# One layer of a hybrid decoder: norm chains and transformed operands issued in small steps between products, gate and up results moved to VectorE, weight sums to GpSimd

## The chip, the cores and the metric

One core of a Trainium2 chip runs the whole program. The metric is device microseconds of that core for one execution, the median of three runs. TensorE (PE) does the matrix products, VectorE (DVE), ScalarE (ACT) and GpSimd (POOL) the elementwise work, and SyncE's queue (SP) issues every DMA.

## The reference

One decoder layer on 1088 tokens (a prompt of 1024 and 8 sequences of 8 new tokens), model width 1024, in float32. Cut to what matters here:

```python
mix = concat([o_att, o_ssm]) @ w_out          # 2048 -> 1024
x = x + rmsnorm(mix, g_post_mix)
f = rmsnorm(x, g_pre_ffn)
f = (silu(f @ w_gate) * (f @ w_up)) @ w_down  # 1024 -> 2816 -> 1024
x = x + rmsnorm(f, g_post_ffn)
```

Ahead of it stand one combined input projection, sliding-window attention with sinks and a Mamba-2 scan with a gated group norm. The change touches none of those but the group norm of the last tokens.

## The kernel before, in words

Activations lie transposed, features on partitions and tokens along the free axis, in three chunks of 384, 384 and 320 tokens (CH). Each float32 operand is split into a high part (an ACT copy that rounds) and a low part (a subtraction on POOL or DVE), and each product is three matmuls (high by high, high by low, low by high).

PE's order is the order in which the program is written out: generators yield the PE time that they want to see pass, in microseconds of matmul columns, and `weave` hands out that much of a filler (the big products) before it goes on with the mixer. The other engines' queues and SP's are ordered by a planner from the same program: an operation goes out when it can, by priority of its place in the program, and `high_priority` moves it ahead. Each queue then runs strictly in its order.

The stages that matter here, in order:

- **Attention, out-projection op(0), op(1), op(2)** (L1000): one product per chunk and 128 features, 61 us for a chunk of 384 columns at the pace that the generators count.
- **gate(2)** (L953): the gated group norm of chunk 2. After a gap of 18 us, `rms` sums squares with matmuls by a column of ones (`g2st`), takes the power on POOL, builds a diagonal on DVE (`g2d`), and after a gap of 5.0 broadcasts it with matmuls (`g2R`).
- **chain(c)** (L1029) for each chunk: `rms` over the mixer's result (`pm`), eight k-steps on 128 features (scale L1039, add of x L1040, store to DRAM, square and sum), a gap of 21.76, a second `rms` (`pf`). Chunks 0 and 1 meet in chain(1): the gate and up products of the two are computed by Strassen-Winograd, seven half-size products in place of eight. Its operands B11, B21, B22 and T1 to T4 are built and split there (L1063 to L1083). Chunk 2 is multiplied plainly: chain(2) splits its operand f2.
- **first_up** (L1314), the filler while chain(1) and chain(2) run: `gu_early` gives the B11 and B21 products of the column pairs 0 to 2 (names eg.., eu..), then whole column pairs without their chunk-2 part until chain(2) is done. `part` counts those.
- **gu_unit** (L1140): one block of gate or up weights. It loads four quarter blocks (r11, r21, r22, r12; four raw slots in all), forms the sums S1 to S4 of them (`ssum`; S3 and S4 stand behind the T1 product), splits each (`lot`), and accumulates the products in the banks pa, pb, pc (Winograd) and qa, qb (plain). The bank pb takes T2, T3 and T4 in turn: before each of the last two, DVE must have added the bank into u2 or u3 (L1206, L1227). Results 1 and 2 are added and multiplied by POOL for the larger part (L1228, L1231).
- Then the pairs without chunk-2 part get it (`wino=False`), with h loaded back for **down** (L1345), and **fin(c)** (L1359) norms, adds x and stores.

Of the kernel before, what the change touches and what calls it, by code (L numbers as in the profile page):

```python
# [16 lines left out]
P = 128  # L17
# [18 lines left out]
def hybrid_layer(ctx, tc, A):  # L36
# [145 lines left out]

    def rms(groups, n, inv, name, gap, keep=None):

# [17 lines left out]
        for q in range(len(groups)):  # L202
            Rp = ps("o", name + "R")
            for b, off in enumerate(bl):
                t.matmul(Rp[:, off:off + P], lhsT=ones, rhs=dgs[q][:, b, :], start=True, stop=True)
            with tc.high_priority():
                if keep is None:
                    R = sp.tile([P, n], F32, tag="rs_R", bufs=2, name=name + "R")
                else:
                    R = sp.tile([P, n], F32, name=name + "Rk")  # L210
                    keep.append(R)
                s.copy(R, Rp[:, :n])
                Rs.append(R)
            if q + 1 < len(groups):
                yield 0.51
# [736 lines left out]

    def gate(c, gap=6.0):  # L953

# [15 lines left out]
        yield gap  # L970
        Rs = yield from rms([[Z.t[:, 0, :]] for Y, Z in yz], n, 1.0 / 512, "g%d" % c, 5.0)
        S = Split.__new__(Split)
# [56 lines left out]
    def chain(c, mt, acc, kp):  # L1029
        c0, n = CH[c]  # L1030
        yield 6.8
        R, = yield from rms([[acc]], n, 1.0 / DM, "pm%d" % c, 4.0)
        acc = kp.tile([P, n], F32, tag="acc1", bufs=1, name="acc1")
        acc2 = kp.tile([P, n], F32, tag="acc2", bufs=1, name="acc2")
        for k in range(8):
            xr = kp.tile([P, n], F32, tag="xr", bufs=2, name="xr")
            dma(xr, A["xT"][:, k, c0:c0 + n])
            e, a = (g, acc2) if k % 2 else (v, acc)
            v.scalar_tensor_tensor(mt[:, k, :], mt[:, k, :], vec[:, V_GPM + k:V_GPM + k + 1], R, ALU.mult, ALU.mult)  # L1039
            e.tensor_add(mt[:, k, :], mt[:, k, :], xr)  # L1040
            dma(x2_scr[:, k, c0:c0 + n], mt[:, k, :])
            sumsq(a, mt[:, k, :], k // 2, n, e)
        if c == 1:
            for q, name in enumerate(("B11", "B21")):
                h, l = Half(0, name + "h"), Half(0, name + "l")
                slots[name] = (h, l)
                hilo(name, h.t, l.t)
                for k in range(4):
                    split(h.t, l.t, k, mix[0][:, 4 * q + k, :], g)
            done.add("B1")  # L1050
        yield 21.76
        R, = yield from rms([[acc, acc2]], n, 1.0 / DM, "pf%d" % c, 6.8)

# [7 lines left out]
        elif c == 1:  # L1061
# [6 lines left out]
            for k in range(4):  # L1068
                v.tensor_sub(t1[:, k, :], scaled(k), m0[:, k, :])
            for k in range(4):  # L1070
                split(h.t, l.t, k, scaled(4 + k), g)
                v.tensor_sub(t3[:, k, :], mt[:, 4 + k, :], mt[:, k, :])
                v.tensor_sub(t2[:, k, :], mt[:, 4 + k, :], t1[:, k, :])
                g.tensor_sub(t4[:, k, :], m0[:, 4 + k, :], t2[:, k, :])
            while "op2" not in done:
                yield 1.0
            for name, x, e in (("T2", t2, v), ("T1", t1, v), ("T3", t3, g), ("T4", t4, v)):
                h, l = Half(c, name + "h"), Half(c, name + "l")
                slots[name] = (h, l)
                hilo(name, h.t, l.t)  # L1080
                for k in range(0, 4, 2):
                    s.copy(h.t[:, k:k + 2, :], x[:, k:k + 2, :])
                    e.tensor_sub(l.t[:, k:k + 2, :], x[:, k:k + 2, :], fr(h.t[:, k:k + 2, :]))  # L1083
        else:
            h, l = [fpool.tile([P, 8, n], F32R, tag="F", bufs=3, name="f2" + j) for j in "hl"]
            for k in range(8):
                split(h, l, k, scaled(k), g if k % 2 else v)
            for q in range(2):
                hilo("F%d" % q, h[:, 4 * q:4 * q + 4], l[:, 4 * q:4 * q + 4])
# [50 lines left out]
    def gu_unit(gp, src, j, up, sgs, wino, plain):  # L1140
# [4 lines left out]
        with tc.high_priority(offset=500):  # L1145
            for q, i in ((11, 0), (21, 0), (22, 1), (12, 1)) if wino else ((11, 0), (12, 1), (22, 1), (21, 0)):
                r[q] = wp.tile([P, 4, P], F32, tag="raw", bufs=4, name="%sr%d" % (nm, q))
                wdma[0] = dma(r[q], src[2 * j + q // 20][:, 4 * i:4 * i + 4, :]).ins

        def ssum(i, x, y, sub):  # L1150
            with tc.high_priority(offset=500):
                S[i] = gp.tile([P, 4, P], F32, tag="sraw", bufs=4, name="%sS%d" % (nm, i))
                (v.tensor_sub if sub else v.tensor_add)(S[i], x, y)

# [7 lines left out]
        def out(i, m, c, e, put):  # L1162

            c0, nc_ = CH[c]
            with tc.high_priority():
                if not up:
                    sg = gp.tile([P, nc_], F32, tag="sg2" if c == 2 else "sg", bufs=2 if c == 2 else 4, name=nm + "sg")
                    x = put(sg)
# [16 lines left out]
        if wino:  # L1185
            pa, pb, pc = ps("mm", nm + "pa") if j not in early else None, ps("s", nm + "pb"), ps("t", nm + "pc")
            ssum(1, r[21], r[22], False)
            ssum(2, S[1], r[11], True)
        pre = j in early
        if plain or not pre:  # L1190
# [10 lines left out]
        if wino:  # L1201
# [8 lines left out]
            with tc.high_priority():  # L1210
                s.copy(p5, pc[:, :n])
            ssum(3, r[11], r[21], True)
            ssum(4, r[12], S[2], True)
        if plain or not pre:
# [7 lines left out]
        if wino:  # L1222
# [3 lines left out]
            with tc.high_priority():  # L1226
                v.tensor_add(u3, p1, pb[:, :n])  # L1227
            out(1, 1, 1, g, add(g, u3, p5, u3))  # L1228
            w = lot(S[4], "s4", v)
            yield from prod(pc, n, w, "B22")  # L1230
            out(2, 0, 1, g, add(v, u2, pc[:, :n], u2))  # L1231
        w = lot(r[22], 22)
# [68 lines left out]
    def gate2():  # L1301
        while "op0" not in done:
            yield 1.0
        yield from gate(2, 18.0)

    with pool("chain") as kp:
# [3 lines left out]
        with pool("xl") as xl, pool("gu") as gp:  # L1310
# [27 lines left out]
            for j in range(part[0] + 1):  # L1338
                run(gu_pair(gp, j, wino=False))
                next(hl)  # L1340
                next(hl, None)
            run(hl)

    with pool("down") as dp:
# [14 lines left out]
        def fin(c, Y, accs):  # L1359
            c0, n = CH[c]  # L1360

            def x2_load(m):
                x2 = dp.tile([P, n], F32, tag="x2", bufs=4, name="x2_%d" % m)
                dma(x2, x2_scr[:, m, c0:c0 + n])
                return x2
            x2 = [x2_load(m) for m in range(4)]
            R, = yield from rms([accs], n, 1.0 / DM, "fin%d" % c, 0.0)
            for m in range(8):
# [3 lines left out]
                dma(A["o_y"][:, m, c0:c0 + n], xv)  # L1372
                if m < 4:
                    x2.append(x2_load(m + 4))

        fi = None
        for c, (c0, n) in enumerate(CH):
            Y = dp.tile([P, 8, n], F32, tag="Y", bufs=2, name="Y%d" % c)
            accs = [sp.tile([P, n], F32, tag="acc", bufs=2, name="acc")]
            for m in range(8):  # L1380
# [5 lines left out]
                if m == 2 and c < 2:  # L1386
                    run(h_load(dp, c + 1, range(3), c == 0))
                with tc.high_priority():
                    s.copy(Y[:, m, :], o[:, :n])
                    if c == 2 and m > 5:  # L1390
                        accs.append(stage(n, "sq"))
                        s.activation(accs[-1], Y[:, m, :], AF.Square)
                    else:
                        sumsq(accs[0], Y[:, m, :], m, n, v if c == 2 else g)
            for h in held[c]:
                h.free()
            if c < 2:
                run(h_load(dp, c + 1, range(3, 6), c == 1))
            fi = fin(c, Y, accs)
        finish(fi)  # L1400
# [115 lines left out]
```

## Time and profile before

| | |
|---|---|
| median of three runs | 1731.97 us (1728.89 to 1734.25) |
| the profiled execution's own time | 1738.02 us |
| its span, first to last instruction | 1736.1 us |
| busy in the span: PE, POOL, DVE, ACT | 1615.1, 864.4, 964.6, 754.3 us |
| mean granted clock of PE | 0.967 of full speed |

Rows of the profile are of that one execution. A wait is named by the engine that ended it. The granted clock has two levels, 1.2 and 2.4 GHz, shown as 0.5 and 1.0 of full speed; a mean between them is a mixture in time.

### The profile page before, as it was taken

The numbers are of one execution on the slowest core, as the hardware profiler recorded it, in microseconds if no ns is written. First come the engines' busy times: TensorE is split into PE (matmuls) and PEld (weight loads), VectorE is DVE, ScalarE is ACT, GpSimd is POOL, SyncE is SP. The second block draws the span as 40 slices with busy tenths as digits, with TensorE's granted clock in tenths as the row PEclk, the third lists the DMA queues.
The fourth block names the chain that finished last, engine by engine and source line by source line (L and its number), as shares of the span: only waits on it lengthen the run. The fifth ranks groups of instructions, "written<-read, shape, count | busy, mean of one in ns | idle before, by whom it ended". The sixth has DMA issues, their size and how long they took to land.

```text
span 1736.1 us, 27321 instructions
## 1 busy us (share of the span) xinstructions
PE 1615.1 (93%) x9695; PEld 1516.1 (87%) x9695; DVE 964.6 (56%) x1807; ACT 754.3 (43%) x1602; POOL 864.4 (50%) x682
## 2 busy tenths in 40 slices
PE   9999999999789989898996879999999999999996
PEld 6889988878677867898996769999999999999996
DVE  6796768663588878355568743333333342144242
ACT  5242344431576676454544323333333344453442
POOL 5462366665553343234558545444444455556563
PEclk9999999999999999988998989999999999999998
DMA  5122565565552341543463432222222257566463
GB/s 186 32 85 101 152 171 154 151 189 189 147 156 81 93 144 57 167 149 118 130 196 95 134 123 85 75 75 75 73 77 75 75 160 223 157 207 203 143 200 103
DMA packets 180832, 226.10 MB, mean 130 GB/s; under 512 B 21784, under 2 KB 122136, under 8 KB 180664
## 3 DMA queue, kind: packets, MB, share of 16 engines
q1 hardware_dynamic: 180696, 224.37, 41.8%
q8 instruction: 76, 1.25, 0.3%
q14 instruction: 60, 0.49, 0.1%
HBM read 177.99 MB, written 48.54 MB: 130 GB/s over the span
## 4 chain that ended last, share of the span: by engine, by line
PE 58%; DVE 9%; POOL 5%; issue 4%; DMA 4%; ACT 3%; SPq 1%; POOLq 0%; DVEq 0%; ACTq 0%
PE od L1356 5%; PE od L1354 5%; PE od L1355 5%; PE ip L131 2%; PE op L131 2%; PE ip L132 2%; PE ip L133 2%; PE op L133 2%; PE op L132 2%; DMA xr<-in_xT 1%; DVE a_0S L742 1%; DVE gy L982 1%; PE a_0o L820 1%; DMA hs<-h_scr 1%; DVE a_1S L794 1%
## 5 line engine op out<-in xcount | busy, mean ns | idle before, releaser
L115 POOL TENSOR_TENSOR wi_1l<-wi_1r,wi_1h 128x512 fp32r<-128x512 f32 x40 | 56.1, 1405 | 72.5 <-ACT wi_1h L114 67.2
L115 POOL TENSOR_TENSOR wi_0l<-wi_0r,wi_0h 128x512 fp32r<-128x512 f32 x40 | 58.3, 1460 | 31.0 <-ACT wi_0h L114 28.4
L115 POOL TENSOR_TENSOR wos_1l<-wos_1r,wos_1h 128x512 fp32r<-128x512 f32 x24 | 33.5, 1397 | 55.9 <-ACT wos_1h L114 46.0
L115 POOL TENSOR_TENSOR woa_1l<-woa_1r,woa_1h 128x512 fp32r<-128x512 f32 x24 | 33.9, 1412 | 52.5 <-ACT woa_1h L114 50.6
L115 DVE TENSOR_TENSOR wd_2l<-wd_2r,wd_2h 128x512 fp32r<-128x512 f32 x24 | 20.0, 832 | 67.3 <-ACT wd_2h L114 63.3
L115 POOL TENSOR_TENSOR wd_3l<-wd_3r,wd_3h 128x512 fp32r<-128x512 f32 x24 | 33.2, 1383 | 46.0 <-ACT wd_3h L114 43.4
L131 PE MATMUL ip<-x1h,wi_0h 128*128 128x384 f32 x128 | 48.0, 375 | 5.1 <-DVE cbuf L362 2.8
L375 DVE SCALAR_TENSOR_TENSOR cacc<-cbuf,vec,cacc 128x1112 f32<-128x1112 f32 x36 | 52.3, 1455 | 0.7
L131 PE MATMUL ip<-x0h,wi_0h 128*128 128x384 f32 x128 | 48.2, 377 | 4.2 <-DVE cbuf L362 3.5
L115 POOL TENSOR_TENSOR wd_0l<-wd_0r,wd_0h 128x512 fp32r<-128x512 f32 x24 | 32.6, 1358 | 32.8 <-ACT wd_0h L114 32.8
L133 PE MATMUL ip<-x0h,wi_0l 128*128 128x384 f32 x128 | 44.3, 346 | 1.5 <-POOL wi_0l L115 1.5
L1017 DVE TENSOR_TENSOR acc<-acc,sq 128x384 f32<-128x384 f32 (+1 forms) x35 | 27.2, 778 | 32.7 <-ACT sq L1016 32.3
L131 PE MATMUL ip<-x0h,wi_1h 128*128 128x384 f32 x128 | 45.3, 354 | 0.0
L131 PE MATMUL ip<-x1h,wi_1h 128*128 128x384 f32 x128 | 44.5, 347 | 0.0
L133 PE MATMUL ip<-x1h,wi_0l 128*128 128x384 f32 x128 | 44.2, 345 | 0.0
L132 PE MATMUL ip<-x0l,wi_0h 128*128 128x384 f32 x128 | 44.1, 344 | 0.0
L132 PE MATMUL ip<-x1l,wi_0h 128*128 128x384 f32 x128 | 44.0, 343 | 0.0
L133 PE MATMUL ip<-x0h,wi_1l 128*128 128x384 f32 x128 | 43.3, 338 | 0.0
L132 PE MATMUL ip<-x0l,wi_1h 128*128 128x384 f32 x128 | 43.3, 338 | 0.0
L133 PE MATMUL ip<-x1h,wi_1l 128*128 128x384 f32 x128 | 43.1, 337 | 0.0
L132 PE MATMUL ip<-x1l,wi_1h 128*128 128x384 f32 x128 | 43.1, 337 | 0.0
L115 DVE TENSOR_TENSOR wd_5l<-wd_5r,wd_5h 128x256 fp32r<-128x256 f32 x24 | 17.3, 721 | 45.1 <-ACT wd_5h L114 45.1
(2821 smaller groups left out, 6511.5 us busy)
## 6 DMA issues: line engine op xcount, KB each, us to landing
wi_0r<-in_w_in SPq DMA_DIRECT2D x40, 256.0 KB
wi_1r<-in_w_in SPq DMA_DIRECT2D x40, 256.0 KB
hs<-h_scr SPq DMA_DIRECT2D x22, 384.0 KB
wos_0r<-in_w_os SPq DMA_DIRECT2D x24, 256.0 KB
wos_1r<-in_w_os SPq DMA_DIRECT2D x24, 256.0 KB
woa_0r<-in_w_oa SPq DMA_DIRECT2D x24, 256.0 KB
woa_1r<-in_w_oa SPq DMA_DIRECT2D x24, 256.0 KB
wd_0r<-in_w_d SPq DMA_DIRECT2D x24, 256.0 KB
```

What stands on the lines that cost most here:

```text
L115: (eng or g).tensor_sub(lo, raw, fr(hi))
L131: t.matmul(out, lhsT=wh, rhs=xh, start=k == 0, stop=False)
L132: t.matmul(out, lhsT=wh, rhs=xl, start=False, stop=False)
L133: t.matmul(out, lhsT=wl, rhs=xh, start=False, stop=k == n - 1)
L375: v.scalar_tensor_tensor(acc[:, :L], buf[:, k:k + L], vec[:, cw + k:cw + k + 1], acc[:, :L], ALU.mult, ALU.add)
L742: v.tensor_scalar_mul(w, w, den[:, h:h + 1])
L794: v.tensor_tensor_reduce(Sms[e][:, gi, :W], sq_[:, a, :W], cst[:, mcol:mcol + W], 1.0, -3.0e38, ALU.add, ALU.max, mx[:, h:h + 1])
L820: t.matmul(op[HD * e:HD * e + HD, :], lhsT=VT[:, HD * e:HD * e + HD], rhs=PTs[e], start=kt == 0, stop=kt == nk - 1)
L1017: e.tensor_add(acc, acc, sq)
L1354: t.matmul(o[:, :n], lhsT=wh, rhs=xh, start=q + k == 0, stop=False)
L1355: t.matmul(o[:, :n], lhsT=wh, rhs=xl, start=False, stop=False)
L1356: t.matmul(o[:, :n], lhsT=wl, rhs=xh, start=False, stop=q + k == NFF - 1)
```

## The change

The eight k-steps, the building of the T operands and the splits of f2 each get a yield behind them, in place of one gap of 21.76 us; the gaps between the two halves of `rms` are longer for chunk 2. Adds of x for chunks 1 and 2 and the low parts of B22 go from POOL to DVE. In a gate or up unit, results 1 and 2 are added and multiplied on DVE alone, S3 and S4 are formed at the head of the unit on POOL, and r11 and r12 get two slots of their own beside the four. Chunk 2's x is loaded in two pieces during `down`, its last norm factor is read from PSUM, and its last two squares are taken from PSUM.

```diff
-    def rms(groups, n, inv, name, gap, keep=None):
+    def rms(groups, n, inv, name, gap, keep=None, direct=False):
...
                 t.matmul(Rp[:, off:off + P], lhsT=ones, rhs=dgs[q][:, b, :], start=True, stop=True)
+            if direct:
+                Rs.append(Rp[:, :n])
+                continue
             with tc.high_priority():
...
-    def gate(c, gap=6.0):
+    def gate(c, gap=6.0, gap2=5.0):
...
         yield gap
-        Rs = yield from rms([[Z.t[:, 0, :]] for Y, Z in yz], n, 1.0 / 512, "g%d" % c, 5.0)
+        Rs = yield from rms([[Z.t[:, 0, :]] for Y, Z in yz], n, 1.0 / 512, "g%d" % c, gap2)
         S = Split.__new__(Split)
...
         yield 6.8
-        R, = yield from rms([[acc]], n, 1.0 / DM, "pm%d" % c, 4.0)
...
+        R, = yield from rms([[acc]], n, 1.0 / DM, "pm%d" % c, 8.0 if c == 2 else 4.0)
         acc = kp.tile([P, n], F32, tag="acc1", bufs=1, name="acc1")
...
             v.scalar_tensor_tensor(mt[:, k, :], mt[:, k, :], vec[:, V_GPM + k:V_GPM + k + 1], R, ALU.mult, ALU.mult)
-            e.tensor_add(mt[:, k, :], mt[:, k, :], xr)
+            (v if c else e).tensor_add(mt[:, k, :], mt[:, k, :], xr)
             dma(x2_scr[:, k, c0:c0 + n], mt[:, k, :])
             sumsq(a, mt[:, k, :], k // 2, n, e)
+            yield 4.5 if c == 2 else 2.7
         if c == 1:
...
             done.add("B1")
-        yield 21.76
-        R, = yield from rms([[acc, acc2]], n, 1.0 / DM, "pf%d" % c, 6.8)
+        R, = yield from rms([[acc, acc2]], n, 1.0 / DM, "pf%d" % c, 10.0 if c == 2 else 6.8)
...
                 v.tensor_sub(t1[:, k, :], scaled(k), m0[:, k, :])
+                yield 1.2
             for k in range(4):
-                split(h.t, l.t, k, scaled(4 + k), g)
+                split(h.t, l.t, k, scaled(4 + k), v)
                 v.tensor_sub(t3[:, k, :], mt[:, 4 + k, :], mt[:, k, :])
...
                 g.tensor_sub(t4[:, k, :], m0[:, 4 + k, :], t2[:, k, :])
+                yield 2.5
             while "op2" not in done:
...
                     e.tensor_sub(l.t[:, k:k + 2, :], x[:, k:k + 2, :], fr(h.t[:, k:k + 2, :]))
+                    yield 1.2
         else:
...
                 split(h, l, k, scaled(k), g if k % 2 else v)
+                yield 2.0
             for q in range(2):
...
             for q, i in ((11, 0), (21, 0), (22, 1), (12, 1)) if wino else ((11, 0), (12, 1), (22, 1), (21, 0)):
-                r[q] = wp.tile([P, 4, P], F32, tag="raw", bufs=4, name="%sr%d" % (nm, q))
...
+                r[q] = (wp.tile([P, 4, P], F32, tag="raw", bufs=4, name="%sr%d" % (nm, q)) if q > 20 else
+                        gp.tile([P, 4, P], F32, tag="rawx", bufs=2, name="%sr%d" % (nm, q)))
                 wdma[0] = dma(r[q], src[2 * j + q // 20][:, 4 * i:4 * i + 4, :]).ins
...
-        def ssum(i, x, y, sub):
+        def ssum(i, x, y, sub, e=v):
             with tc.high_priority(offset=500):
                 S[i] = gp.tile([P, 4, P], F32, tag="sraw", bufs=4, name="%sS%d" % (nm, i))
-                (v.tensor_sub if sub else v.tensor_add)(S[i], x, y)
+                (e.tensor_sub if sub else e.tensor_add)(S[i], x, y)
...
                 if not up:
-                    sg = gp.tile([P, nc_], F32, tag="sg2" if c == 2 else "sg", bufs=2 if c == 2 else 4, name=nm + "sg")
+                    sg = stage(nc_, nm + "sg") if c == 2 else gp.tile([P, nc_], F32, tag="sg", bufs=4, name=nm + "sg")
                     x = put(sg)
...
             ssum(2, S[1], r[11], True)
+            ssum(4, r[12], S[2], True, g)
+            ssum(3, r[11], r[21], True, g)
         pre = j in early
...
                 s.copy(p5, pc[:, :n])
-            ssum(3, r[11], r[21], True)
-            ssum(4, r[12], S[2], True)
         if plain or not pre:
...
                 v.tensor_add(u3, p1, pb[:, :n])
-            out(1, 1, 1, g, add(g, u3, p5, u3))
+            out(1, 1, 1, v, add(v, u3, p5, u3))
             w = lot(S[4], "s4", v)
             yield from prod(pc, n, w, "B22")
-            out(2, 0, 1, g, add(v, u2, pc[:, :n], u2))
+            out(2, 0, 1, v, add(v, u2, pc[:, :n], u2))
         w = lot(r[22], 22)
...
             yield 1.0
-        yield from gate(2, 18.0)
+        yield from gate(2, 18.0, 9.0)
...
                 run(gu_pair(gp, j, wino=False))
-                next(hl)
+                next(hl, None)
                 next(hl, None)
...
                 return x2
-            x2 = [x2_load(m) for m in range(4)]
-            R, = yield from rms([accs], n, 1.0 / DM, "fin%d" % c, 0.0)
+            if c < 2:
+                x2 = [x2_load(m) for m in range(4)]
+            else:
+                x2 = []
+                for q in range(2):
+                    x_ = Half(c, "x2h%d" % q, F32)
+                    dma(x_.t, x2_scr[:, 4 * q:4 * q + 4, c0:c0 + n])
+                    x2 += [x_.t[:, k, :] for k in range(4)]
+                yield
+            last = c == 2
+            R, = yield from rms([accs], n, 1.0 / DM, "fin%d" % c, 0.0, direct=last)
             for m in range(8):
...
                 dma(A["o_y"][:, m, c0:c0 + n], xv)
-                if m < 4:
+                if m < 4 and c < 2:
                     x2.append(x2_load(m + 4))
...
                     run(h_load(dp, c + 1, range(3), c == 0))
+                if m == 3 and c == 2:
+                    fi = fin(c, Y, accs)
+                    next(fi)
                 with tc.high_priority():
-                    s.copy(Y[:, m, :], o[:, :n])
                     if c == 2 and m > 5:
                         accs.append(stage(n, "sq"))
-                        s.activation(accs[-1], Y[:, m, :], AF.Square)
+                        s.activation(accs[-1], o[:, :n], AF.Square)
+                        v.tensor_copy(Y[:, m, :], o[:, :n])
                     else:
+                        s.copy(Y[:, m, :], o[:, :n])
                         sumsq(accs[0], Y[:, m, :], m, n, v if c == 2 else g)
...
                 run(h_load(dp, c + 1, range(3, 6), c == 1))
-            fi = fin(c, Y, accs)
+            if c < 2:
+                fi = fin(c, Y, accs)
         finish(fi)
```

## Rows read from the trace of the kernel before

**Rows 1.** Busy time by stretch: stretch, length, then per engine busy time (instructions), granted clock, DMA.
```profile
745.00:826.00 81.00, 74.89 (x410) 71.07 (x408) 47.02 (x102) 40.59 (x87) 33.51 (x25) 0.85 0.40 127
826.00:915.00 89.00, 85.40 (x551) 84.56 (x550) 57.08 (x76) 44.63 (x87) 51.54 (x40) 0.98 0.51 162
915.00:1069.00 154.00, 119.00 (x632) 113.80 (x632) 97.96 (x122) 53.83 (x104) 95.22 (x72) 0.91 0.34 110
1069.00:1390.00 321.00, 321.00 (x1953) 320.88 (x1952) 122.73 (x177) 105.10 (x193) 148.34 (x119) 1.00 0.24 77
1390.00:1450.00 60.00, 56.56 (x350) 56.24 (x350) 20.66 (x26) 28.03 (x47) 33.87 (x26) 0.94 0.56 170
```

**Rows 2.** PE's waits from 915 to 1069 us: total us, times, longest.
```profile
PE u1pc L1107 <- ACT u1ws4h L1098: 8.5, 1, 8.5
PE eu00pa L1107 <- ACT mix L1008: 5.9, 1, 5.9
PE g1pc L1107 <- ACT g1ws4h L1098: 3.2, 1, 3.2
PE eu01pa L1107 <- DVE eg10sg L1135: 3.2, 1, 3.2
PE pm2R L205 <- DVE pm2d L199: 2.4, 2, 1.8
...
PE eu00pa L1107 <- ACT e L1130: 1.9, 1, 1.9
...
PE eu02pa L1107 <- ACT e L1130: 0.2, 1, 0.2
```

**Rows 3.** PE's longest wait from 745 to 915 us.
```profile
PE g2R L205 <- DVE g2d L199: 4.7, 3, 3.3
```

**Rows 4.** Busy time by stretch: the 5 us behind PE's longest wait.
```profile
1022.00:1027.00 5.00, 5.00 (x15) 4.77 (x16) 3.72 (x5) 1.22 (x3) 2.52 (x2) 0.50 0.35 112
```

**Rows 5.** The chain that ended last: start, us, what; a Winograd and two plain products.
```profile
1069.19 2.11 PE g3pa L1107 x12
...
1087.36 3.52 PE g3qb L1107 x24
```

**Rows 6.** SP's queue in order of time, around its wait for POOL.
```profile
1016.36 0.33 SPq L1174 DMA_DIRECT2D h_scr<-g1sg  x1
1016.74 0.43 SPq L1148 DMA_DIRECT2D u1r<-in_w_u  x1
```

**Rows 7.** ACT in order of time: start, us, operation, idle time before and releaser.
```profile
920.00 0.51 ACT L1026 CAST B22h<-mix 128x384 fp32r<-128x384 f32 x1 [4.75 <-DVE mix L1055]
...
922.81 0.42 ACT L1008 COPY mix<-op 128x320 f32<-128x320 f32 x1
```

**Rows 8.** Durations by line: ns min/median/max, first and last start.
```profile
L1039 DVE SCALAR_TENSOR_TENSOR mix<-mix,vec,pm2R x8: 534/544/1579, 947.2 to 960.4; 128x320 f32<-128x320 f32 x8
L1153 DVE TENSOR_TENSOR g1S<-g1r,g1r x2: 678/682/686, 973.1 to 977.7; 128x512 f32<-128x512 f32 x2
L1227 DVE TENSOR_TENSOR u1u<-e,u1pb x1: 555/555/555, 1013.6 to 1013.6; 128x384 f32<-128x384 f32 x1
L1099 POOL TENSOR_TENSOR g1w22l<-g1r,g1w22h x2: 1277/1286/1296, 1000.7 to 1433.8; 128x512 fp32r<-128x512 f32 x2
L1173 POOL TENSOR_TENSOR g1sg<-g1sg,u1u x2: 993/1230/1468, 1015.3 to 1029.2; 128x384 f32<-128x384 f32 x2
```

**Rows 9.** The chain that ended last, in the program's last 20 us.
```profile
1722.28 0.43 ACT fin2R L212
...
1727.20 1.90 DMA out_o_y<-x
1729.19 2.35 DMA x<-x_scr
...
1732.34 0.89 POOLq L1512
```

**Rows 10.** The chain that ended last: the first of eight plain products behind the Winograd pairs.
```profile
1422.61 3.52 PE g0qa L1107 x24
```

## The prediction

> **What bounds the kernel now.** I read the busy time by stretch first. Between 1069 and 1390 us PE is busy for all of its 321 us at full clock, with DVE at 122.73 and POOL at 148.34 us: there PE is the bound, and nothing that lightens another engine can gain. In the stretch before it, 915 to 1069, PE is busy for 119.00 of 154.00 us at a mean clock of 0.91, while DVE (97.96) and POOL (95.22) are at 62 to 64% [rows 1]. So this stretch is bound by waits, not by any engine's work. PE's waits there name them: 15 entries from 8.5 us down to 0.2, and they add up to the missing 35.0 us [rows 2]. Between 745 and 915 the largest is 4.7 us for the diagonal of gate(2) [rows 3].
>
> A wait costs more than itself. After u1pc's wait, which ends at 1022, the granted clock is 0.50 to 1027 [rows 4]: PE works at 1.2 GHz for some us after it has stood still. What the work of 915 to 1069 needs at full clock can be counted. A Winograd product takes 2.11 us from start to start there (call it 2.1), two plain ones on one weight bank pair 3.52, so 1.76 each [rows 5]. The stretch holds 12 early products, 20 of pairs 0 and 1, 10 of pair 2 and its 8 plain ones: 42 x 2.1 + 8 x 1.76 = 102.3 us, and with about 3 us of norm matmuls (my estimate) 105. Of the 49 us lost, 35.0 are waits and 14 the low clock (119.00 busy against 105).
>
> **The change, part by part.** All other work of PE keeps its size: the same products are done, only some chunk-2 parts come later. How many can be worked out from the yields. Before, chain(2) asks for 6.8 + 4.0 + 21.76 + 6.8 = 39.4 us of filler after op(2); the early products give 23.0 by the generators' count (12 x 1.92) and a pair 19.2, so one pair is woven in. After, chain(1) asks for 6.8 + 4.0 + 8 x 2.7 + 6.8 + 4 x 1.2 + 4 x 2.5 = 54.0 against op(2)'s 51.2, and 8 x 1.2 = 9.6 more for the T splits; chain(2) then asks for 6.8 + 8 + 8 x 4.5 + 10 + 8 x 2 = 76.8. It ends 2.8 + 9.6 + 76.8 = 89.2 us behind op(2), after 23.0 + 3 x 19.2 = 80.6, inside pair 3. So four pairs are woven, pair 4 follows without its plain part, and five pairs instead of two get it at the end. Chain(2)'s DVE work, which now meets one pair, is spread over four.
>
> (a) *The early products.* eu00pa waits for the last copy of op(2) out of PSUM, which is ACT's at 922.81; ahead of it in ACT's queue stands a B22 cast that had stood idle for 4.75 us on a scaling by DVE [rows 7]. The T building gets in the way of what PE needs. Its low parts of B22 go to DVE and its steps fall behind the weights' splits by priority, and chain(2)'s first norm comes some 12 us later. I take the early stretch's 11.2 us of waits (5.9, 3.2, 1.9, 0.2) down to 3. POOL stays busy there: 12 low parts at 1.29 us [rows 8] are 15.5 us in some 25, so I don't take zero. The B1 splits, now written behind 21.6 us of gap, have 19 us left to op(2)'s end for 8 copies and 8 low parts of about 1 us: hidden. Were the T operands themselves late, the wait would move to g0pb.
>
> (b) *Longer gaps.* pm2R's 2.4 us [rows 2] have 4 us more of cover, and so has gate(2)'s g2R with 4.7 [rows 3]: both to zero. I add 1.3 us for the clock behind g2R: 6.0 for 745 to 915. That stretch's other losses (3.6 us of idle time from 826, 1.4 of the 6.1 before it [rows 1]) I leave.
>
> (c) *Units while chain(2) runs.* u1pc's 8.5 us: the store of g1sg waits in SP's queue until 1016.36 for POOL's multiplication, and the load of u1r comes out behind it at 1016.74 [rows 6]; that quarter block becomes S4, which the next product needs. After the change r11 and r12 have their own slots, their sums are formed at the head of the unit, so the load can go out most of a unit earlier, and the store's producer is DVE's 0.555 us in place of POOL's 1.0 to 1.5 [rows 8]. The 3.2 us of g1pc are of the same kind. All these waits (21.2 us, the 35.0 less (a) and pm2R) I take down to 7, because DVE will be full. Per pair without chunk-2 part it then does 8 operations of 512 columns at 0.68 and 13 of 384 at 0.555 [rows 8], 12.7 us in 10 products of 2.1, 60%; chain(2)'s two k-steps per 9 us add five at 0.54, 27%. POOL has 6 low parts and 4 sums at about 1.29, 12.9 in 21, 61%. Each k-step's load and store of x also enter SP's queue among the units' loads, and a store that waits for DVE there holds the weights behind it. Nearly nine tenths on an in-order engine that must empty pb within the next product (2.1 us) will not run without waits.
>
> (d) *Clock.* With 10 of 35 us of waits left, and most of them short, I take the 14 us to 4. So (a) to (d) leave 14 of the 49 us in 915 to 1069: a gain of 35, by bounds 15 (only SP's wait, pm2R and their clock go) to 49.
>
> (e) *The end.* The factor needs no ACT copy (0.43 us), and the last square, now taken from the bank, no copy of like size before it [rows 9]. The later x tiles were loaded only when an output store had left: a 1.90 us store, then 2.35 us for x, landed at 1731.54; now they lie there. From 1721.85 on DVE does 8 scalings and 4 adds at 0.54 [rows 8], 6.5 us, the last POOL add takes 0.9 and the last store 2.9 (1733.2 to 1736.1 [rows 9]): end at 1732.2, a gain of 3.9; bounds 2 to 5. The two loads in `down` and DVE's two copies hide under PE's products.
>
> (f) *Costs at nothing.* Three more pairs load and split their weights twice: six units of four blocks of 256 KB, 6.3 MB, and 14 splits; they hide under the 70 us of the last plain products (ten units at 7.04). Without that cover 6.3 MB at the 170 GB/s of 1390 to 1450 [rows 1] would be 37 us. From 1069 on full units trade two DVE sums for POOL's and two POOL results for DVE's; PE's full 321 us cover it. The 3.4 us without PE from 1390 to 1450 [rows 1] fall where h is loaded back, which stays where it was: no gain, at best 5 with the clock.
>
> **Sum.** 35 + 6.0 + 3.9 = 45, from 1738.0 to 1693. That execution lies 6.0 us over the median of 1731.97, so the prediction is 1687. By the bounds, gains run from 15 + 0 + 2 = 17 (1715) to 49 + 17 (745 to 826 at full clock without waits: 81 less 74.89 x 0.85 [rows 1]) + 5 + 5 = 76 (1656).
>
> **Rivals.**
> *Only part goes* (0.17). The planner starts chain work when it is ready, not where it is written, so the yields move PE's order and priorities alone, DVE's and POOL's queues stay as tangled, and T operands come late. Then what goes is the SP wait and its like (11.7), the two gaps (7.1), clock (6) and the end (3.9): 29, so 1703, or with chain waits grown again 15 to 25, so 1707 to 1717. For it: early low parts and T steps still share POOL. Against: 12 us more room before chain(2).
>
> *The shared port* (0.07, slower). A DVE operation with both inputs in SBUF takes 0.54 us alone and 1.58 at worst, one POOL operation longer, while one that reads a bank takes 0.555 [rows 8]. POOL now runs two sums more in each of the 22 units, beside DVE operations that gain SBUF-only adds and multiplications. If u3's add stands behind such a one (1.6 + 0.555 + hand-over) it passes the 2.1 us of cover. It decides from about 1 us lost at each of the two reuses of pb in a unit: 44 us take the gain, and with the low clock at half of them, 60, the time is 1747. Against it: in 1069 to 1390 such collisions are there already and PE never waits. The Trainium skill, "SBUF — State Buffer", section "Who interferes with whom", has the rule: a DVE instruction with two SBUF inputs contends with a GpSimd one that reads SBUF, and whichever comes second is blocked fully. By that rule the trace agrees (the 1.04 us more), and each sum moved to POOL is a block of some 1.3 us for DVE.
>
> *The plain end can't be fed* (0.06, slower). Before, only eight halves of 3.52 us ran there, with no wait [rows 10]; now twenty do. If SP's stores hold each unit's loads, as at 1016, each unit waits for some 5 us: 50 us, 1737. It decides from 4.5 us per unit. Against: a unit's four blocks, 1.05 MB in 7.04 us, are 149 GB/s, under the 170 of 1390 to 1450 [rows 1].
>
> *All of it goes* (0.08): 1656 to 1670, if DVE keeps up and PE's clock never falls.
>
> **How the numbers follow.** The forecast, 1671 to 1705, has 0.57; part 0.17; all 0.08; the slower ones 0.13; within the 0.3% (5 us) that a measurement can tell, 0.05. Faster is 0.57 + 0.17 + 0.08 = 0.82. The range of 1663 to 1720 leaves out the slower cases and the tip of the best.
>
> **What would show it.** PE's busy share in the stretch from op(2)'s end to the first full unit at 0.9 or more, and no wait there over 2 us; no load of r12 behind a store; stores and loads of x gone from the last 8 us. Wrong would be: DVE at 95% with PE waiting for u2 or u3, waits of the plain end, or T operands late at the first product of pair 0.

## The result, and the profile after

The changed kernel takes 1714.11 us (median of 5 runs, 1710.70 to 1722.79) beside 1734.25 for the kernel before (5 runs on the same chip): a ratio of 0.9898, 95% interval 0.9878 to 0.9918. The forecast was 1687. So the sign was right, and the gain less than half of the 45 us forecast.

The two profiled executions have spans of 1736.1 and 1712.3 us. Three marks divide the 23.8 us between them: the first early product (eg00pa), the first T2 product (g0pb), and the last matmul of `down`. The marks carry some spread of their own: the profile before lies 3.8 us above its median, and the first matmul of op(0), ahead of which none of the edits stands, starts anywhere from 612.7 to 616.7 us in the fourteen profiles (615.4 before, 614.2 after).

| stretch | before | after | gain | forecast |
|---|---|---|---|---|
| start to eg00pa | 915.1 | 903.2 | 11.9 | 6.0 |
| eg00pa to g0pb | 45.5 | 39.8 | 5.7 | 35 for this row and the next |
| g0pb to the last matmul of `down` | 755.5 | 753.9 | 1.6 | |
| last matmul of `down` to the end | 20.0 | 15.4 | 4.6 | 3.9 |

The busy time by stretch of the changed kernel, cut at those marks and where the full units begin (1095), answers to [rows 1]; its columns are the same:

```profile
745.00:826.00 81.00, 79.63 (x473) 77.09 (x472) 57.50 (x113) 44.44 (x95) 39.58 (x28) 0.94 0.48 154
826.00:903.00 77.00, 74.20 (x487) 73.64 (x486) 50.88 (x71) 39.23 (x78) 41.60 (x34) 0.98 0.53 167
903.00:943.00 40.00, 29.93 (x153) 29.29 (x152) 29.35 (x26) 18.57 (x34) 31.51 (x21) 0.87 0.32 102
943.00:1095.00 152.00, 132.00 (x724) 128.67 (x723) 102.25 (x143) 55.83 (x108) 89.54 (x68) 0.96 0.37 122
1095.00:1337.00 242.00, 242.00 (x1475) 242.00 (x1474) 85.96 (x132) 81.62 (x150) 115.44 (x89) 1.00 0.24 75
1337.00:1430.00 93.00, 90.14 (x591) 89.83 (x590) 26.18 (x35) 41.11 (x70) 60.21 (x45) 0.98 0.64 195
```

From 745 to 826 the clock is 0.94 where it was 0.85, and PE stands still for 1.4 us in place of 6.1. The plain end (1337 to 1430) runs at 195 GB/s with PE busy for 97%. What is left is in the third and fourth row. PE's waits there, from eg00pa to the first full unit, answer to [rows 2]:

```profile
PE eu00pa L1115 <- ACT e L1138: 6.3, 1, 6.3
PE eu00pa L1115 <- ACT mix L1011: 3.8, 1, 3.8
PE g0pb L1115 <- DVE g0u L1237: 3.5, 1, 3.5
PE g1pb L1115 <- ACT sq L1019: 3.5, 1, 3.5
PE u4pa L1115 <- POOL u4w11l L1107: 3.2, 1, 3.2
PE u4pa L1115 <- ACT u4w11h L1106: 1.7, 1, 1.7
PE g3pb L1115 <- DVE g3u L1218: 1.7, 1, 1.7
PE u0pb L1115 <- DVE u0u L1237: 1.6, 1, 1.6
PE u3pb L1115 <- DVE u3u L1237: 1.5, 1, 1.5
PE u2pb L1115 <- DVE u2u L1237: 1.2, 1, 1.2
PE g2pb L1115 <- DVE g2u L1237: 1.1, 1, 1.1
PE u3pa L1115 <- ACT u3p L1210: 0.9, 1, 0.9
```

The 8.5 and 3.2 us of u1pc and g1pc are gone, as forecast. In their place stand six waits for a bank that DVE has yet to empty (10.6 us), two at the head of u4 (4.9) and two that end with ACT (4.4): 19.9 us from the third line down, where 21.2 were to fall to 7. The first two lines, 10.1 us, are the early products', where 11.2 were to fall to 3. The longest of all, 6.3 us, is for the copy `e` of a bank that eu00pa's next product needs. In ACT's queue it stands behind two casts of T operands, and the first of them had waited 6.96 us for DVE:

```profile
919.45 0.83 ACT L1088 CAST T2h<-mix 128x768 fp32r<-128x768 f32 x1 [6.96 <-DVE mix L1078]
...
920.92 0.47 ACT L1138 COPY e<-eu00pa 128x384 f32<-128x384 f32 x1
```

That subtraction of DVE's starts only at 917.26, behind low parts of T2, B22 and T1. It is the pattern of [rows 7], with a cast of T2 in place of one of B22.

How a wait for a bank arises is to be seen in DVE's timeline ahead of g0u L1237, for which PE stood until 955.8:

```profile
950.19 0.69 DVE L1163 TENSOR_TENSOR g1S<-g1r,g1r 128x512 f32<-128x512 f32 x1 [3.15 <-DMA g1r<-in_w_g]
950.80 1.79 DVE L1107 TENSOR_TENSOR u0ws1l<-u0S,u0ws1h 128x512 fp32r<-128x512 f32 x1
952.62 0.69 DVE L1163 TENSOR_TENSOR g1S<-g1S,g1r 128x512 f32<-128x512 f32 x1
953.23 2.02 DVE L1043 SCALAR_TENSOR_TENSOR mix<-mix,vec,pm2R 128x320 f32<-128x320 f32 x2
955.16 0.54 DVE L1237 TENSOR_TENSOR g0u<-e,g0pb 128x384 f32<-128x384 f32 x1
```

Three operations of 512 columns and two scalings stand ahead of it. Two of them are stretched: u0ws1l to 1.79 us (its like above and below take 0.69), the two scalings to 2.02 (0.54 each alone [rows 8]). GpSimd was reading SBUF beside both, with a low part from 950.75 and a sum of g1 from 953.44.

Ahead of u4's waits stand, in this order, lines of SP's queue, a row of busy time, and lines of GpSimd:

```profile
1051.11 10.33 SPq L1184 DMA_DIRECT2D h_scr<-g3sg  x4
1061.87 0.82 SPq L1158 DMA_DIRECT2D u4r<-in_w_u  x2
```

```profile
1069.00:1076.00 7.00, 4.35 (x24) 3.71 (x22) 2.95 (x6) 3.64 (x7) 1.94 (x2) 1.00 0.01 2
```

```profile
1074.06 1.28 POOL L1163 TENSOR_TENSOR u4S<-u4r,u4S 128x512 f32<-128x512 f32 x1 [9.87 <-DVE u4S L1163]
1075.30 1.26 POOL L1163 TENSOR_TENSOR u4S<-u4r,u4r 128x512 f32<-128x512 f32 x1
1076.52 1.71 POOL L1107 TENSOR_TENSOR u4w11l<-u4r,u4w11h 128x512 fp32r<-128x512 f32 x1
```

Two loads of u4r, its r11 and r12, still come out behind four stores, as in [rows 6]. But the DMA engines move almost nothing from 1069 on (a share of 0.01), so both had landed by then, and it isn't for them that u4 is late. DVE's sum of u4 (at 1073.24) and ACT's cast of r11 (at 1073.79) stand in their queues directly behind the last result of g4, which waits for g4's T4 product. And u4w11l, which PE waits for longest, stands behind two sums that PE needs only later, and which waited 9.87 us for that sum of DVE's.

### The profile page after: what moved, and what is told of

The parts are those of the page before. It is cut to its first block, busy times and chain, and to the rows that moved or that the text cites. A ratio compares the mean times of both kernels' runs of the same rounds, so it can differ in the third digit from the quotient of the medians.

```text
span 1712.3 us, 27330 instructions
## 1 busy us (share of the span) xinstructions
PE 1608.6 (94%) x9695; PEld 1513.5 (88%) x9695; DVE 965.2 (56%) x1821; ACT 760.0 (44%) x1613; POOL 879.2 (51%) x684
## 5 line engine op out<-in xcount | busy, mean ns | idle before, releaser
L1303 DVE TENSOR_TENSOR Hl<-hs,Hh 128x768 fp32r<-128x768 f32 (+1 forms) x22 | 24.7, 1133 | 32.5 <-ACT Hh L1302 28.5
```

Source lines behind the costliest of these rows:

```text
L1303: v.tensor_sub(l[:, k:k + 2], x, fr(h[:, k:k + 2]))
```

## The experiments

Times are medians, ratios are to the kernel before on the same chip. One measure helps to read all of them: the stretch from the first T2 product (g0pb) to the first full unit (the first one with its chunk-2 part done at once: g3 before, g5 with five pairs woven in), less what PE needs for it. PE needs 2.11 us for a Winograd product and 1.76 for a plain one [rows 5], and I put 1.2 for a norm's matmuls (estimate). Before, that is 30 x 2.11 + 8 x 1.76 + 1.2 = 78.6 us; with pairs 0 to 4 woven in, 58 x 2.11 + 1.2 = 123.6.

| kernel | time, us | ratio, interval | g0pb | full unit | loss there |
|---|---|---|---|---|---|
| before | 1734 | 1 | 960.6 | 1069.0 | 29.8 |
| b_head_dve | 1742.1 | 1.0051 (1.0035 to 1.0066) | 959.0 | 1073.9 | 36.3 |
| a_units_back | 1728.2 | 0.9955 (0.9940 to 0.9971) | 946.6 | 1108.6 | 38.4 |
| a_res_pool | 1718.1 | 0.9910 (0.9892 to 0.9929) | 944.1 | 1099.3 | 31.6 |
| after | 1714.1 | 0.9898 (0.9878 to 0.9918) | 943.0 | 1094.8 | 28.2 |
| a_sums_dve | 1705.8 | 0.9836 (0.9814 to 0.9858) | 945.0 | 1087.3 | 18.7 |
| a_no_s34 | 1697.9 | 0.9791 (0.9759 to 0.9823) | 945.3 | 1080.8 | 11.9 |

**The gap alone.** The kernel before, with the longer gap of gate(2) and nothing else.

```diff
-    def gate(c, gap=6.0):
+    def gate(c, gap=6.0, gap2=5.0):
-        yield from gate(2, 18.0)
+        yield from gate(2, 18.0, 9.0)
```

> The kernel before with one part of the change: gate(2)'s gap between its two halves 9.0 in place of 5.0. Theory: this gap alone brings what was gained up to op(2)'s end (the changed kernel's op(2) ends 11.9 us earlier), because the wait for g2d and the low clock around it go together: 1723 to 1726 against 1734 before, and op(2) ends near 904 us. Rival: the k-steps of chain(0), handed out singly, made most of it; then the gap is worth its 4.7 us of wait at most, 1729 to 1731, and op(2) ends near 910.

Measured: 1725.7 us, ratio 0.9947 (0.9928 to 0.9967). The time is the one that the theory gave, but its first early product comes at 908.9, 6.2 us ahead of 915.1, and so about where the rival put it: the gap isn't all of the 11.9. This smallest edit brings about half of the whole change's gain.

**Chain(2) in one block.** The changed kernel, chain(2)'s steps without their yields, its gaps as before. Three pairs are then woven in, not five.

```diff
-            yield 4.5 if c == 2 else 2.7
+            if c < 2:
+                yield 2.7
+        if c == 2:
+            yield 21.76
-                yield 2.0
```

> The changed kernel with chain(2)'s steps in one block again (gaps 4.0, 21.76, 6.8, no yields between k-steps or splits of f2). By the yields two pairs are then woven in place of four. Theory (DVE full): chain(2)'s work needs DVE's time wherever it stands; in one block it gives DVE one spell of 100%, in small steps several, and PE's loss from g0 to the first full unit stays at 25 to 30 us: 1711 to 1718 against 1714. Rival (small steps are what helps): without them the loss goes back up by 10 us or more, 1722 to 1730. Second rival (each woven unit costs some 2.5 us for standing beside chain(2)): two pairs fewer lose 8 to 10 us less, 1704 to 1708.

Measured: 1712.0 us, 0.9877 (0.9857 to 0.9896): the same as with the steps. That chain(2)'s work is handed out over more pairs is worth nothing by itself.

**The sums' engine.** The changed kernel, with S3 and S4 at the head as there, but on DVE.

```diff
-            ssum(4, r[12], S[2], True, g)
-            ssum(3, r[11], r[21], True, g)
+            ssum(4, r[12], S[2], True)
+            ssum(3, r[11], r[21], True)
```

> The changed kernel with S3 and S4 formed at the unit's head, but on DVE. Theory (DVE full because POOL's operations hold it up): POOL loses 2 operations of 1.3 us a unit and DVE gains 2 of 0.69, so DVE's lengthening by collisions, 29.5 us from 943 to 1095, falls to 20 or less and pays for most of the 14 us of sums in the ten woven units: 1711 to 1718, no change. Rival (it is DVE's own work alone that makes it full): 14 us more on it cost PE 6 to 12 us, 1720 to 1726.

Measured: 1705.8 us, below both expectations. Its row of busy time for the woven stretch, beside the fourth one of the changed kernel above:

```profile
943.00:1095.00 152.00, 138.29 (x780) 134.36 (x779) 119.71 (x170) 58.64 (x113) 68.10 (x50) 0.99 0.40 127
```

DVE is busier by 17 us, GpSimd idler by 21, and PE does 6 us more. I had taken DVE's busy time to be what held PE; this run speaks against it. Ahead of g0u L1237 its timeline reads:

```profile
949.92 0.69 DVE L1107 TENSOR_TENSOR u0ws1l<-u0S,u0ws1h 128x512 fp32r<-128x512 f32 x1
950.65 0.69 DVE L1163 TENSOR_TENSOR g1S<-g1S,g1r 128x512 f32<-128x512 f32 x1
951.56 1.01 DVE L1043 SCALAR_TENSOR_TENSOR mix<-mix,vec,pm2R 128x320 f32<-128x320 f32 x2 [0.22 <-ACT pm2R L215]
952.49 0.55 DVE L1237 TENSOR_TENSOR g0u<-e,g0pb 128x384 f32<-128x384 f32 x1
```

The same operations take 0.69 and 1.01 us in place of 1.79 and 2.02, g0u comes 2.7 us earlier, and PE doesn't wait for it at all. GpSimd stood idle from 949.2 to 952.7 there. u4w11l's 3.2 us are 0.8 there.

**The sums left out.** T3 and B22 take S1 and S2 as their weights, so that S3 and S4 aren't computed.

```diff
-            ssum(4, r[12], S[2], True, g)
-            ssum(3, r[11], r[21], True, g)
+            S[3], S[4] = S[1], S[2]
```

> The changed kernel without the sums S3 and S4: the products T3 and B22 take S1 and S2 as their weights in all units. If these sums hurt by being GpSimd's (its queue, and DVE's operations that meet them): 1699 to 1706, at or below the run with them on DVE (1705.8). Rival, it was only that DVE is full of other work, and leaving out GpSimd's sums frees nothing: 1711 to 1715.

Measured: 1697.9 us. So the two sums cost some 16 us on GpSimd and 8 on DVE (the intervals of the two overlap a little).

**The results' engine.** The changed kernel, with results 1 and 2 of a unit on GpSimd as before.

```diff
-            out(1, 1, 1, v, add(v, u3, p5, u3))
+            out(1, 1, 1, g, add(g, u3, p5, u3))
-            out(2, 0, 1, v, add(v, u2, pc[:, :n], u2))
+            out(2, 0, 1, g, add(v, u2, pc[:, :n], u2))
```

> The changed kernel with gate and up results 1 and 2 added and multiplied by POOL as before. Theory (DVE full): DVE has some 2 us a pair less and the u adds come earlier, but each POOL operation holds up DVE's SBUF-only ones, so the gain is small: 1708 to 1716. Rival (results on VectorE were the useful part, because the stores and so SP's queue waited for POOL): waits for weights come back, as u1pc's 8.5 us, and it is slower by 6 us or more: 1720 to 1728.

Measured: 1718.1 us, 4 above the changed kernel, with overlapping intervals: this part helps little if at all.

**The units as before.** The changed kernel with the unit edits undone: four raw slots, the sums in the middle on DVE, results 1 and 2 on GpSimd (not in the lines shown).

```diff
-                r[q] = (wp.tile(...) if q > 20 else gp.tile([P, 4, P], F32, tag="rawx", bufs=2, ...))
+                r[q] = wp.tile([P, 4, P], F32, tag="raw", bufs=4, name="%sr%d" % (nm, q))
-            ssum(4, r[12], S[2], True, g)
-            ssum(3, r[11], r[21], True, g)
...
+            ssum(3, r[11], r[21], True)
+            ssum(4, r[12], S[2], True)
```

> The changed kernel with its units as before: four raw slots, S3 and S4 in the middle of a unit on DVE, and two results of each unit on GpSimd. What is left of the change is the chains' steps, the longer gaps, four woven pairs and the end. By the prediction's step (c) the waits behind SP's stores are back in four pairs: 1722 to 1735. Rival, the gain never came from the units: 1708 to 1716.

Measured: 1728.2 us, so the units' edits together are worth 14. Its largest waits in the woven stretch:

```profile
PE g4pb L1115 <- ACT g4ws2h L1106: 6.7, 1, 6.7
PE g1pb L1115 <- DVE g1u L1215: 5.1, 1, 5.1
...
PE g3pb L1115 <- DVE g3u L1215: 4.5, 1, 4.5
```

The first is of the kind that step (c) names: three loads of g4r come out behind stores of g3sg, and DVE's sum of g4, from which g4ws2h is made, stands idle for them. The next two are waits for a bank that DVE has yet to empty.

```profile
1059.01 8.13 SPq L1183 DMA_DIRECT2D h_scr<-g3sg  x4
1067.23 1.38 SPq L1157 DMA_DIRECT2D g4r<-in_w_g  x3
```

```profile
1071.21 0.69 DVE L1162 TENSOR_TENSOR g4S<-g4r,g4r 128x512 f32<-128x512 f32 x1 [5.39 <-DMA g4r<-in_w_g]
```

And the kernel is no faster than the gap alone (0.9947): what the chains' steps gain ahead of op(2)'s end, the five woven pairs lose again.

**The sums at the head alone.** The kernel before, with six slots and all four sums at the head on DVE; chunk 2's `sg` is a `stage` tile, for room.

```diff
+            ssum(4, r[12], S[2], True)
+            ssum(3, r[11], r[21], True)
...
-            ssum(3, r[11], r[21], True)
-            ssum(4, r[12], S[2], True)
```

> The kernel before with one part of the change: six raw slots, and all four sums at the unit's head, on DVE. The chain keeps its steps and only one pair is woven in. By the prediction's step (c), the waits for u1r and g1r behind SP's stores go, with the low clock after them: 1719 to 1724. Rival, other waits of DVE or ACT take their place: 1729 to 1735.

Measured: 1742.1 us, slower than the kernel before and than both expectations. u1pc's and g1pc's waits are gone, and the first line of PE's waits is a new one, of chain(2)'s norm:

```profile
PE pf2st L191 <- DVE acc L1017: 12.6, 1, 12.6
```

Ahead of that operation DVE stood idle for a load of x. In SP's queue a load of u1r had waited for GpSimd for 8.2 us, to 977.0, and only behind it came the stores and loads of chain(2)'s last k-steps:

```profile
968.39 8.95 SPq L1149 DMA_DIRECT2D u1r<-in_w_u  x2
...
978.34 0.49 SPq L1037 DMA_DIRECT2D xr<-in_xT  x1
...
984.20 0.92 SPq L1037 DMA_DIRECT2D xr<-in_xT  x2
```

```profile
986.55 0.49 DVE L1040 TENSOR_TENSOR mix<-mix,xr 128x320 f32<-128x320 f32 x1 [6.90 <-DMA xr<-in_xT]
```

So a wait that goes can hand its time to the next one in the in-order queues: the weights' loads held back the chain's, and the norm's sums, which PE meets in a fixed place, were late.

**A bank for T3, and the factor in PSUM.** Both kernels have all sums on DVE. In the first, T3 of the woven units has a bank of its own and isn't added to T2's, so that u3 lacks T2 and the last quarter T3; the second also leaves the factors of chains 1 and 2 in PSUM.

```diff
+            pd = pb if plain else ps("o", nm + "pd")
-            yield from prod(pb, n, w, "T3")
+            yield from prod(pd, n, w, "T3", not plain)
```

> All four sums of a unit on DVE (1705.8 us in the run before this one), and in the woven units T3 gets a bank of its own, so that T3 doesn't wait for u2's add out of pb and T4 has a whole product more of cover. If the waits that are left are the reuse of pb (4.35 us for T4 and 4.1 us for T3 in that run's waits): 1697 to 1702. Rival, DVE's queue as a whole is what is late and the wait only moves to the next bank that DVE must empty: 1704 to 1708.

```diff
-        ... "pm%d" % c, 8.0 if c == 2 else 4.0)
+        ... "pm%d" % c, 8.0 if c == 2 else 4.0, direct=c > 0)
-        ... "pf%d" % c, 10.0 if c == 2 else 6.8)
+        ... "pf%d" % c, 10.0 if c == 2 else 6.8, direct=c > 0)
```

> As a_sd_t3, and the norm factors of chain(1) and chain(2) are read from their PSUM bank instead of an SBUF copy, so that DVE's scalings have one SBUF input and can't collide with GpSimd. If collisions of these scalings matter (some 3 us over their 0.54 us in the early products and the woven units): 2 to 4 us below a_sd_t3. Rival, they are hidden: equal within 1.5 us. Second rival, the factor's bank is held through eight k-steps and T3 and the next norms want one of the same banks: 3 to 10 us above a_sd_t3.

Measured: 1700.3 us, 0.9824 (0.9791 to 0.9856), and 1695.1, 0.9780 (0.9759 to 0.9800). The first interval holds most of a_sums_dve's, so it isn't shown that the bank alone gains; in the profiles the loss in the woven stretch is 13.4 us for 18.7. The step to the second is 5 us, with intervals that overlap a little; there the loss is 12.4, so most of the step lies ahead of g0pb. What it does to DVE's scalings is plain; minimum, median and longest of the same instructions in ns, first with the factor in SBUF (a_sd_t3), then in PSUM (a_sd_t3_r):

```profile
L1043 DVE SCALAR_TENSOR_TENSOR mix<-mix,vec,pm2R x8: 539/542/1146, 950.4 to 976.7; 128x320 f32<-128x320 f32 x8
...
L1059 DVE SCALAR_TENSOR_TENSOR mix<-mix,vec,pf1R x8: 605/613/1732, 891.1 to 906.2; 128x384 f32<-128x384 f32 x8
L1059 DVE SCALAR_TENSOR_TENSOR mix<-mix,vec,pf2R x8: 540/774/1575, 1009.1 to 1026.1; 128x320 f32<-128x320 f32 x8
```

```profile
L1043 DVE SCALAR_TENSOR_TENSOR mix<-mix,vec,pm2R x8: 534/536/540, 945.8 to 971.6; 128x320 f32<-128x320 f32 x8
...
L1059 DVE SCALAR_TENSOR_TENSOR mix<-mix,vec,pf1R x8: 600/602/615, 888.4 to 901.9; 128x384 f32<-128x384 f32 x8
L1059 DVE SCALAR_TENSOR_TENSOR mix<-mix,vec,pf2R x8: 534/538/548, 1003.4 to 1020.8; 128x320 f32<-128x320 f32 x8
```

Not one of these 24 is stretched any more, though eleven of them ran beside a GpSimd operation for all or part of their time.

**B22's low parts back on GpSimd**, with all sums on DVE.

```diff
-                split(h.t, l.t, k, scaled(4 + k), v)
+                split(h.t, l.t, k, scaled(4 + k), g)
```

> All four sums of a unit on DVE, and B22's low parts back on GpSimd, as before the change. If DVE, busy for all of 896 to 926 us, is what makes the two waits of the early products (3.8 and 6.3 us): 1701 to 1704. Rival, GpSimd (14 of 15 us busy there) then makes the early weights' low parts late: 1707 to 1713.

Measured: 1708.1 us, 0.9853 (0.9827 to 0.9879). The early products take 43.6 us from eg00pa to g0pb, and 41.0 with these parts on DVE. The wait of 6.3 us for `e` falls to 1.4, but the one for `mix` rises from 3.8 to 5.9 and others come (2.4 for eg11sg, 1.5 for eg01l on GpSimd). So moving these four parts gains nothing; whether they held PE where they were, the run doesn't show.

**A version that computes the reference.** u3 is formed from u2 and T3's bank, and T4 starts T2's bank afresh; sums on DVE and factors in PSUM as above.

```diff
-                v.tensor_add(u3, p1, pb[:, :n])
+                v.tensor_add(u3, p1 if plain else u2, pd[:, :n])
...
-            yield from prod(pb, n, w, "T4")
-            out(3, 1, 0, v, add(v, p1, pb[:, :n], p1))
+            yield from prod(pb, n, w, "T4", not plain)
+            out(3, 1, 0, v, add(v, p3, pb[:, :n], p3))
```

> All four sums of a unit on DVE, the norm factors of chain(1) and chain(2) read from their PSUM bank, and in the woven units T3 in a bank of its own, with u3 formed from u2 and T4 begun afresh in T2's bank, so that the whole of the reference is computed. The same work for each engine as in a_sd_t3_r (1695.1 us): 1692 to 1698. Rival, the last quarter now hangs on u3, and T4 waits again: 1699 to 1705.

Measured: 1699.9 us, 0.9802 (0.9780 to 0.9825). Some 5 us of a_sd_t3_r are lost again, in the profile at pair 4. The last kernel adds a gap ahead of the T splits:

```diff
             while "op2" not in done:
                 yield 1.0
+            yield 8.0
```

> As best, with 8 us more asked for ahead of the T splits, which in a_sd_t3_r take DVE 15 us without a break from 906.8 to 922 while the T operands are used from 939 on. If these splits, ahead in the queues of DVE and ACT, make the early products wait (3.4 us for e, 4.0 for eg10sg): 4 to 8 us below best. Rival, chain(2) and the T operands come late in their turn, or POOL's early low parts are what holds: within 2 us of best, or above it.

Measured: 1697.5 us, 0.9783 (0.9760 to 0.9806), not to be told from the one without the gap. The waits that it was made for stay at 3.4 and 4.0 us, for on DVE nothing moved:

```profile
907.91 1.76 DVE L1090 TENSOR_TENSOR T2l<-mix,T2h 128x768 fp32r<-128x768 f32 x1
...
923.21 0.54 DVE L1144 TENSOR_TENSOR eg10sg<-eg10sg,eu00pa 128x384 f32<-128x384 f32 x1
```

Without the gap T2l began at 906.84, in the same place of the queue, and that whole execution stood 1.1 us earlier (eg00pa at 901.0 and 902.1). What did move is chain(2), by 11 us (its first scaling from 945.9 to 956.9). Here a yield moved what was late; work that was ready went where the engine looked free. Both versions beat the changed kernel's 0.9898 with intervals well apart.

## Why the prediction was right and wrong

**The bound** was read rightly: PE is held by waits between op(2)'s end and the first full unit, and a shorter list of waits there is time gained, as a_sums_dve and a_no_s34 show.

**(b)** was right for what it counts and too small for its stretch: 11.9 us in place of 6.0. Counted from the first matmul of op(0), eg00pa comes after 299.7 us before, 293.4 with the gap alone (b_gap2), 290.5 in a_chain2_block and 289.1 in the changed kernel. So the gap gives 6.3 where 6.0 was forecast for it. Another 3 to 4 come with what a_chain2_block keeps, the steps of chains 0 and 1 and the adds moved to DVE among it, which no run separates; the prediction left the stretch's other losses as they were, at no gain. The rest, 1.2, lies ahead of op(0) and is spread.

**(a) failed.** "I take the early stretch's 11.2 us of waits (...) down to 3": 10.1 us are left. The reason given there, that T building gets out of the way of what PE needs, does not hold: it was only written later, not queued later (best_t shows how little a yield moves it), and T2's cast still stands ahead of `e` in ACT's queue. Reading the factor from PSUM shortens this stretch by 2 us (40.7 to 38.7) and the way from op(0) to eg00pa by 3 to 5; T2's cast then waits 3.8 us in place of 7.0, and PE 3.4 for `e` in place of 6.3 (best). What the rest would be worth isn't settled: T2's cast, and on DVE the splits of T1, T2 and T4, 15 us without a break ahead of eg10sg, stand in the way in the timelines, but no run moved them.

**(c) is the step that cost most.** "All these waits (...) I take down to 7, because DVE will be full." The mechanism at SP was right, and its waits went. But 19.9 us of other waits took their place. The prediction counted DVE's busy share, 60% and 27%, and took the waits from that. The share was no guide: at 67% (102.25 of 152 us) PE lost 28.2 us, at 79% 18.7. What counted, where the timelines show it, is what stands ahead of the one operation that PE waits for, and how long that takes: sums on GpSimd put 1.3 us and more into its own in-order queue ahead of a low part, and beside DVE's sums and scalings. Moving two sums to GpSimd therefore cost 8 us of the units' gain, and leaving them out would give 8 more. How much of the 8 is GpSimd's queue and how much the stretched operations, the runs don't separate: with the sums on DVE, the excess of all DVE operations over the shortest of their line and shape, summed from 943 to 1095, is 33 us and not less than the 30 with them on GpSimd. It falls on others.

**(d) fell with (a) and (c).** Of the loss of 28.2 us in the woven stretch after, 19.9 are waits and 8 the low clock and the rest; before, 21.4 and 8. So the clock gave nothing back there: its mean is 0.96, and 0.99 only with the sums on DVE or left out.

**(e)** gained 4.6 for 3.9. The chain of the tail, with no load and no copy of the factor in it, answers to [rows 9]:

```profile
1697.12 0.45 ACT sq L1413
1697.61 1.74 PE fin2st L191 x14
...
1700.94 1.63 PE fin2R L205 x6
1702.60 1.01 DVE Y L1389 x2
...
1706.32 1.04 POOL x2h L1390
```

**(f)** held: five plain parts stand at the end, fed at 195 GB/s, with no wait over 0.5 us but u10pb's 2.9 and 1.3 us for weights of `down`; HBM reads are 6.3 MB more, as computed.

**The signs** that were named came out against the forecast: PE is busy for 0.84 of the stretch from eg00pa to the first full unit (161.9 of 192.0 us), not 0.9, five of its waits are over 3 us where none was to pass 2, and u4's r12 is still loaded behind stores. Of the signs of being wrong, none came: DVE is at 67%, not 95%, the plain end has no waits, and the T operands are there at the first product of pair 0. The failure was one that the prediction had not named a sign for.

**The rivals.** "Only part goes" named 1703 to 1717 and is what happened in size: SP's waits, the gaps and the end went, and the T operands' steps stayed tangled. The shared port was taken too lightly as a mechanism and too heavily as a price. It didn't turn the sign, but sums on GpSimd do cost time, and a scaling with both inputs in SBUF took up to 1732 ns where the same one with an input in PSUM never took over 615. The Trainium skill, "SBUF — State Buffer", "Who interferes with whom", says that a DVE instruction with at most one SBUF input, outside the two-port modes, does not contend with GpSimd; the 24 scalings shown for a_sd_t3_r, 534 to 615 ns, agree.

## What to carry to other kernels

When a wait on the path goes, ask what stands next in each in-order queue: sums at the head alone (b_head_dve), or the chain's steps, gaps and tail without the units' edits (a_units_back, no better than the gap alone), lost what they had won. Don't put small work on a slower engine just because it is idle; look at what stands behind it in that engine's queue, and which DVE operations run beside it. An operand that DVE can read from PSUM as it lies there saves the copy and the collision.

## What the runs showed that I had not expected

A busier engine gave a shorter time: DVE went from 102.25 to 119.71 us of the same 152, and PE's loss there from 28.2 to 18.7. Eight scalings whose factor lies in PSUM took 534 to 548 ns, all of them, where the same eight spread from 540 to 1575 with it in SBUF. And 8 us of filler asked for ahead of the T splits left them within 1.2 us of where they had been, and moved the chain behind them by 11. The longest new wait of b_head_dve, 12.6 us, came from loads of x behind a load of weights, in a kernel changed only to bring the sums forward.
